# Products of the modulation weights and sums of the head norms in other places, and all low halves of the weights on VectorE for the middle of a hybrid attention block

## The chip, the cores and the metric

The kernel runs on one core of a Trainium2 chip. TensorE does the matmuls (PE in the profile, PEld its weight loads), VectorE (DVE), ScalarE (ACT) and GpSimd (POOL) work on tiles, and SyncE (SP) issues nearly all transfers. The metric is device time in microseconds, the median of several runs. The profile is that of one further execution.

## The reference

One layer of a diffusion backbone over 256 latent tokens and 256 context tokens, width 2048, all in float32:

```python
sh1, sc1, g1, sh2, sc2, g2 = split(silu(c) @ w_ada + b_ada, 6)        # and the same of c_ctx
h_l = modulate(rms_norm(x, norm1_w), sh1, sc1)                        # h_c from ctx
gq, gk, gv, gr, gaf, gab, dq, dk, dv = split(h @ w_in)                # for both token sets
ya = rms_norm(gla_scan(...)) * silu(gr)                               # gated linear attention, both directions
yb = rms_norm(diff_softmax(rope(rms_norm(dq)), [rms_norm(dk_c), rope(rms_norm(dk_l))], dv))
g_a, g_b = split(sigmoid(h_l @ w_gate + b_gate))
x = x + g1 * ((g_a * (ya @ w_proj_gla) + g_b * (yb @ w_proj_diff)) @ w_out)
h2 = modulate(rms_norm(x, norm2_w), sh2, sc2)
x = x + g2 * ((silu(gate) * val) @ w_down)       # gate, val = split(depthwise_conv3(h2 @ w_up))
```

`w_ada` is 2048 x 12288. Its first third (`sh1`, `sc1`) is needed at the start, `g1` at the output projection, `sh2` and `sc2` behind it, `g2` at the very end.

## The kernel before, in words

Activations lie transposed, channels on the 128 partitions. To keep float32 precision on TensorE every operand is written as a high half (the value rounded to the matmul's format) and a low half (the value less the high half), and three products are added: high x high, high x low and low x high.

**Weights.** `fetch` (line 224) loads 1024 columns of 128 rows, 512 KB, into one of four `wraw` buffers through SP. `split` (line 197) makes the halves of 512 of these columns: ScalarE copies the high half into `whi` (line 206), then the low half `wlo` is a subtraction (line 213) on VectorE, or on GpSimd for every `splits[1]`-th split. Each kind of half has four buffers. `splits[1]` is 0 in the first sweep, then 4 (`PSH` and `PSH2`, lines 39 and 40) for all the rest.

**Tiles.** `col_tile` (line 238) makes one 128-column tile of a weight times the 256 latent tokens: two fetches, four splits, and for each split a quad of four wide matmuls (`h0` to `h3`, 512 columns, high and low halves of the activations side by side, line 262) and four narrow ones with the low half of the weight (`l0` to `l3`, 256 columns, line 264). `col_tile2` does the same for both token sets with six matmuls per 128 rows, and `row_tile` (lines 275 to 277) puts the tokens on the partitions for the values.

**Modulation products.** The last two thirds of `w_ada` are not multiplied on TensorE. `ada_load` (line 326) brings 128 pieces of 128 x 1024 through SP, in program order, into two `araw` buffers, and `ada_dot` (line 334) multiplies one by the condition row and adds it up on VectorE (line 336). `ada_next(n)` (line 650) adds n to what is due and, for each whole piece due, does the oldest product when both buffers are taken, then loads the next. `ada_dot` is ordered behind VectorE's last low half, and VectorE works in order: a product whose weights have not landed holds up what stands behind it. `ada_done(j0)` (line 663) sees to it that the sixteen columns from j0 are finished.

**Norms of heads.** `heads_norm` (line 597) squares a finished query or key tile and appends the rest of its work to `later`; `flush` runs it when the next tile is at its second fetch. This rest splits the squares with `split`, adds them up over a head with two matmuls (`sums`, lines 594 and 595, tile `hss`) and normalizes.

**Stages**, with times of the profile: the first sweep (to 142 us); gated linear attention with its queries, keys and values and the other branch's keys (to 419); the value chunk 0 (`dv_chunk`, sixteen row splits with twelve matmuls each, tile `dvb`), four query tiles (`dq_tile`), the value chunk 1 (to 553); eight heads of differential attention, with three gate tiles behind each and the other four query tiles between, then eight gate tiles more (`gate_tile`, to 797); sixteen pairs of projection tiles (`pga`, `pgb`, to 886); sixteen output tiles (`mix`, to 978), behind whose half the second modulation begins; the first six up strips (`up`, to 1013), the others (`upg`, `upv`, to 1471), and the down tiles.

The order of the instructions on each engine is not the program's: a planner lays them out by simulated durations, `tc.high_priority` moves attention ahead, and only `tc.keep_in_program_order` and `after` bind.

Of the kernel before, what the change touches and what calls it, by code (L numbers as in the profile page):

```python
# [23 lines left out]
DK = 64  # L24
# [14 lines left out]
PSH2 = 4  # L39
# [1 line left out]
UPS = 6  # L41
SLOTS = 12
EARLY_ADA = 4, 14
GATE_ADA = [0.25] * 24 + [2] * 8
NRM = [(0, 0)] * 2 + [(j, j + 1) for j in range(12)] + [(12, 14), (14, 16)]

_VEC = {}
# [99 lines left out]
def layer_kernel(tc, I, out):  # L147
# [3 lines left out]
    with es:  # L151
# [5 lines left out]
        def acc_bank(name):  # L157
            return ps.tile([P, 512], F32, tag="acc", bufs=4, name=name)
# [33 lines left out]
        copied = [None, None]  # L192
        chain = []
        pin = [False]
        later = []

        def flush():
            while later:
                later.pop(0)()

        def split(raw, n, lows=None):

# [35 lines left out]
        def col_tile(src, acts, b, orders=None):  # L238

            nk = src.shape[1]
            nq = nk // 4
            tied = orders is not None
            orders = orders or [TURN] * (nq - 1) + [ENDED]
            for k0 in range(0, nk, 8):
                kn = min(8, nk - k0)
                if k0:  # L250
                    flush()
                raw = fetch(src[:, k0:k0 + kn, :].rearrange("p a b -> p (a b)"), kn * P)
                for kk in range(0, kn, 4):
                    whi, wlo = split(raw[:, kk * P:(kk + 4) * P], 4 * P)
                    order = orders[(k0 + kk) // 4]
                    for which in order:
                        j = int(which[1])
                        k = k0 + kk + j
                        sl = slice(j * P, (j + 1) * P)
                        first, last = k == 0 and which == "h0", k >= nk - 4 and which == order[-1]  # L260
                        if which[0] == "h":
                            i = PE.matmul(b.rearrange("p (a b) -> p a b", a=2), whi[:, sl], acts[k], start=first, stop=last)  # L262
                        else:
                            i = PE.matmul(b[:, T:], wlo[:, sl], acts[k][:, 1, :], start=False, stop=last)  # L264
                        if tied:
                            if chain:
                                after(i, chain[0])
                            chain[:] = [i]

        def added(dst, b):  # L270
            S.copy(dst, b[:, :T])
# [7 lines left out]
        def rsqrt_parts(y, t, ss, n, table=None):  # L279

            i = S.activation(y, ss, AF.Ln, scale=1.0 / n, bias=epsb)
            if table is not None:
                after(i, table)
            exps.append(S.activation(y, y, AF.Exp, scale=-0.5))
            S.activation(t, y, AF.Square)
            V.scalar_tensor_tensor(t, ss, n * EPS, t, op0=ALU.add, op1=ALU.mult)
# [6 lines left out]
        def normed_by(dst, src, w, y, t, n):  # L293
            V.scalar_tensor_tensor(dst, src, w, y, op0=ALU.mult, op1=ALU.mult)
            V.scalar_tensor_tensor(dst, t, -3.0 * n, dst, op0=ALU.add, op1=ALU.mult)
# [291 lines left out]
        def norm_tiles():  # L587
            return [tp.tile([P, 512], F32, tag=t, name=t) for t in ("nraw", "nsq", "hny")]

        def sums(o, m, sq, halves=None):  # L590

            n = sq.shape[1]
            hi, lo = halves or split(sq, n)
            i = PE.matmul(o, m, lo[:, :n], start=True, stop=False)
            after(PE.matmul(o, m, hi[:, :n], start=False, stop=True), i)

        def heads_norm(b, wname, done, o, sq, y):


            n = o.shape[1]  # L600
            if n == T:
                added(o, b)
                S.activation(sq, o, AF.Square)
            else:
                S.activation(sq, b, AF.Square)
                S.copy(o, b)

            def rest():
                s = acc_bank("hss")
                sums(s[:, :n], bones, sq)  # L610
                rsqrt_parts(y, sq, s[:, :n], DK)
                normed_by(o, o, wname, y, sq, DK)
                done(o)

            later.append(rest)

        def onormed(pool, dst, ob, w, halves=None, copy=V.tensor_copy):

# [54 lines left out]
        with tc.tile_pool(name="gla", bufs=1) as pg:  # L673
# [36 lines left out]
            def col_tile2(src, b):  # L710

                for k0 in range(0, KT, 8):
                    if k0:
                        flush()
                    raw = fetch(src[:, k0:k0 + 8, :].rearrange("p a b -> p (a b)"), 1024)
                    for kk in range(8):
                        if kk % 4 == 0:
                            whi, wlo = split(raw[:, kk * P:(kk + 4) * P], 512)
                        k = k0 + kk
                        both_tile(b, k, whi, wlo, slice(kk % 4 * P, (kk % 4 + 1) * P), k == 0, k == KT - 1)  # L720

            def dk_tile(h):
                ada_next(0.5)
# [167 lines left out]

            dk_done(0, sweep[6])
            flush()
            S.copy(gaT, gb[:96, :])
            V.tensor_tensor(gaT[32:64], gb[32:64, :], gaT[32:64].bitcast(F32), op=ALU.subtract)

# [26 lines left out]
        with tc.tile_pool(name="diff", bufs=1) as pd:  # L923
# [11 lines left out]
            def dv_chunk(j):  # L935
                banks = [acc_bank("dvb") for _ in range(4)]

                turn = [6, 7, 0, 1, 2, 3, 4, 5] if j else list(range(8))
                for q in turn:
                    if q == turn[1]:  # L940
                        flush()
                    raw = fetch(I["w_dv"][j, q].rearrange("p a b -> p (a b)"), 1024)
                    ada_next(2)
                    for a in range(2):
                        whi, wlo = split(raw[:, a * 512:(a + 1) * 512], 512)
                        k = 2 * q + a
                        for t in range(4):
                            hi, lo = H[t // 2]
                            row_tile(banks[t], k, whi, wlo, slice(0, 512), hi, lo, slice((t % 2) * P, (t % 2 + 1) * P),
                                     k == 2 * turn[0], k == 2 * turn[-1] + 1)  # L950
                for t in range(4):
                    S.copy(dv[:, t, 512 * j:512 * (j + 1)], banks[t])
# [76 lines left out]
                V.tensor_tensor(gates[j], b[:, T:], gates[j], op=ALU.add)  # L1029

            nts = norm_tiles()
            dv_chunk(0)
            for h in range(4):
                dq_tile(h)
# [43 lines left out]
        for c in range(KT):  # L1078
            ba, bb = acc_bank("pga"), acc_bank("pgb")
            col_tile(I["w_proj"][c, :, 0:8, :], yap, ba)  # L1080
            col_tile(I["w_proj"][c, :, 8:16, :], ybp, bb)
            for j in (c, 16 + c):
                sigs.append(S.activation(gates[j], gates[j], AF.Sigmoid))
                after(sigs[-1], sigm)
                after(sigs[-1], copied[0])
            for b, j in ((ba, c), (bb, 16 + c)):
                t = p3.tile([P, T], F32, tag="pt", bufs=2, name="pt")
                i = added(t, b)
                (G if j > c else V).tensor_tensor(gates[j], t, gates[j], op=ALU.mult)
                if j == c and c:  # L1090
                    merged(c - 1, i)
            ada_next(11 / 16)
        merged(KT - 1, i)
        splits[1] = PSH2
        ada_done(0)


# [19 lines left out]
        half = KT // 2  # L1117
        for c in range(KT):
            b = acc_bank("mix")
            col_tile(I["w_out"][c], A, b)  # L1120
            if c == half:
                ada_done(16)
                ada_done(32)
                V.tensor_scalar(a2, adav[:, 32:48], 1.0, None, op0=ALU.add)
                V.tensor_tensor(a2, a2, vcol("norm2", 0, 16), op=ALU.mult)
                V.tensor_scalar(a2, a2, -0.5 / D, None, op0=ALU.mult)
            xr = p3.tile([P, T], F32, tag="xr", bufs=2, name="xr")
            nc.scalar.dma_start(xr, I["xl"][:, c, :])
            x1.append(C[c][:, 0, :])
            V.scalar_tensor_tensor(xr, b[:, :T], adav[:, c:c + 1], xr, op0=ALU.mult, op1=ALU.add)  # L1130
            i = V.scalar_tensor_tensor(x1[c], b[:, T:], adav[:, c:c + 1], xr, op0=ALU.mult, op1=ALU.add)
            if c >= half:
                for k in range(2 * (c - half), 2 * (c - half) + 2):
                    unnormed(k, i, summed)
            sq = p3.tile([P, T], F32, tag="sq2" if c else "sq_sum", bufs=2 if c else 1, name="sq2")
            S.activation(sq, x1[c], AF.Square)
            if c == 0:
                sq_sum = sq
            elif c < KT - 1:
                summed = G.tensor_tensor(sq_sum, sq_sum, sq, op=ALU.add)  # L1140
# [42 lines left out]

        with tc.tile_pool(name="ffn", bufs=1) as pf:
            gs = []
            ada_buffers(st, 2)
            temps = [0]

# [66 lines left out]
```

## Time and profile before

| What | us |
|---|---|
| median of three runs (1722.74 to 1723.88) | 1723.04 |
| the profiled execution | 1721.52 |
| its span, first to last instruction | 1719.7 |
| TensorE busy | 1687.4 |
| VectorE busy | 1231.6 |
| ScalarE busy | 981.2 |
| GpSimd busy | 487.8 |

The page's lines give busy time, share of the span and the number of instructions. A matmul's end is modelled, so TensorE's 98% says that it seldom stops, not that it runs at its peak. In the groups a line reads: line, engine, operation, out<-in, count, then busy time and mean of one, then the engine's idle time before them and what ended it. In a timeline each row has its start, its length and, in brackets, the idle time ahead of it and who ended that. A row with the engine name SPq is a transfer being issued.

### The profile page before, as it was taken

Reading aid. Unit: us, or ns where it says so; the run is one execution under the profiler, and the core shown is the slowest. Engines: PE = TensorE matmul, PEld = TensorE weight load, DVE = VectorE, ACT = ScalarE, POOL = GpSimd, SP = SyncE. Lnnn points to the kernel's source line nnn. Section 1 sums busy time; section 2 is a strip of 40 time slices with the busy share of each in tenths; the row PEclk is TensorE's granted clock in tenths of the full one; section 3 lists DMA queues with packets and bytes.
Section 4 is the critical chain, followed back from the end, with each engine's and each line's share of the span. In section 5 each row is a group of like instructions: output and inputs, shape, how many; then the busy total and the mean of one; then the engine's idle time right before and its main releaser. Section 6 shows DMA issues by size and latency. Waiting matters only on the chain. (4 is left out here: it accounts for less than half of the span.)

```text
span 1719.7 us, 29261 instructions
## 1 busy us (share of the span) xinstructions
PE 1687.4 (98%) x10460; PEld 1462.9 (85%) x10460; DVE 1231.6 (72%) x2224; ACT 981.2 (57%) x1992; POOL 487.8 (28%) x474
## 2 busy tenths in 40 slices
PE   7999999999999999999999999999999999999999
PEld 5779999897777888878888998888888888888887
DVE  4556655868677888678987898788887777644443
ACT  5335555665355777656665576666666666444443
POOL 0002534645121222223443522222222222222222
PEclk9999999999999999999999999999999999999999
DMA  9995532435766555588776666666766666666664
GB/s 384 408 408 180 173 119 77 136 111 174 242 205 212 172 163 171 171 289 304 246 247 197 187 210 221 226 224 222 232 232 226 225 225 223 207 199 195 196 202 137
DMA packets 108451, 368.75 MB, mean 214 GB/s; under 512 B 12176, under 2 KB 17040, under 8 KB 108304
## 3 DMA queue, kind: packets, MB, share of 16 engines
q1 hardware_dynamic: 103264, 362.51, 63.7%
q10 hardware_dynamic: 5040, 4.37, 0.8%
q8 instruction: 82, 1.34, 0.3%
q14 instruction: 65, 0.53, 0.1%
HBM read 364.73 MB, written 2.10 MB: 213 GB/s over the span
## 5 line engine op out<-in xcount | busy, mean ns | idle before, releaser
L206 ACT CAST whi<-wraw 128x512 fp32r<-128x512 f32 (+2 forms) x1004 | 604.4, 608 | 384.7 <-PE down L262 111.3
L213 DVE TENSOR_TENSOR wlo<-wraw,whi 128x512 fp32r<-128x512 f32 (+2 forms) x761 | 527.9, 703 | 245.0 <-ACT whi L206 239.6
L213 POOL TENSOR_TENSOR wlo<-wraw,whi 128x512 fp32r<-128x512 f32 (+2 forms) x243 | 335.0, 1379 | 932.5 <-ACT whi L206 828.9
L262 PE MATMUL down<-g,whi 128*128 128x512 f32 x704 | 243.6, 392 | 0.0
L262 PE MATMUL upv<-a,whi 128*128 128x512 f32 x656 | 229.2, 392 | 0.0
L262 PE MATMUL upg<-a,whi 128*128 128x512 f32 x656 | 229.2, 392 | 0.0
L336 DVE CUSTOM_DVE_ANT_0 araw<-araw,cb 128x1024 f32<-128x1024 f32 x128 | 178.8, 1400 | 34.7 <-DMA araw<-in_w_ada 34.5
L264 PE MATMUL down<-g,wlo 128*128 128x256 f32 x704 | 195.4, 280 | 0.7 <-DVE wlo L213 0.7
L264 PE MATMUL upv<-a,wlo 128*128 128x256 f32 x656 | 183.1, 280 | 0.6 <-POOL wlo L213 0.3
L264 PE MATMUL upg<-a,wlo 128*128 128x256 f32 x656 | 182.8, 280 | 0.0
L262 PE MATMUL gate<-a,whi 128*128 128x512 f32 x512 | 181.3, 399 | 0.0
L262 PEld LDWEIGHTS down<-g,whi 128*128 128x128 f32 x704 | 131.0, 187 | 28.3
L262 PEld LDWEIGHTS upv<-a,whi 128*128 128x128 f32 x656 | 122.4, 187 | 26.6 <-ACT whi L206 0.2
L262 PEld LDWEIGHTS upg<-a,whi 128*128 128x128 f32 x656 | 122.4, 187 | 26.6
L264 PE MATMUL gate<-a,wlo 128*128 128x256 f32 x512 | 141.3, 286 | 3.1 <-DVE wlo L213 3.1
L264 PEld LDWEIGHTS down<-g,wlo 128*128 128x128 f32 x704 | 132.9, 189 | 1.9 <-DVE wlo L213 1.0
L264 PEld LDWEIGHTS upv<-a,wlo 128*128 128x128 f32 x656 | 123.9, 189 | 2.0 <-DVE wlo L213 0.9
L264 PEld LDWEIGHTS upg<-a,wlo 128*128 128x128 f32 x656 | 123.9, 189 | 1.1 <-DVE wlo L213 0.6
L262 PEld LDWEIGHTS gate<-a,whi 128*128 128x128 f32 x512 | 95.1, 189 | 20.2 <-ACT whi L206 0.8
L264 PEld LDWEIGHTS gate<-a,wlo 128*128 128x128 f32 x512 | 97.1, 190 | 10.1 <-DVE wlo L213 4.5
L262 PE MATMUL mix<-a,whi 128*128 128x512 f32 x256 | 89.0, 397 | 0.7 <-ACT whi L206 0.7
L1197 ACT ACTIVATE C<-C,vec 128x256 f32<-128x256 f32 x88 | 52.6, 598 | 29.1 <-DVE C L272 29.1
(332 smaller groups left out, 3394.2 us busy)
## 6 DMA issues: line engine op xcount, KB each, us to landing
wraw<-in_w_up SPq DMA_DIRECT2D x164, 512.0 KB, 4.4
araw<-in_w_ada SPq DMA_DIRECT2D x128, 512.0 KB, 4.9
wraw<-in_w_down SPq DMA_DIRECT2D x80, 512.0 KB, 3.9
ada<-in_w_ad SPq DMA_DIRECT2D x64, 512.0 KB, 9.9
wraw<-in_w_gate SPq DMA_DIRECT2D x64, 512.0 KB, 4.1
wraw<-in_w_in SPq DMA_DIRECT2D x58, 512.0 KB, 3.9
wraw<-in_w_proj SPq DMA_DIRECT2D x32, 512.0 KB, 4.9
wraw<-in_w_out SPq DMA_DIRECT2D x32, 512.0 KB, 4.2
```

The costliest lines, as they stand in the source:

```text
L206: copied[0] = S.copy(hi[:, :n], raw)
L213: i = e.tensor_tensor(lo[:, :n], raw, hi[:, :n].bitcast(F32), op=ALU.subtract)
L262: i = PE.matmul(b.rearrange("p (a b) -> p a b", a=2), whi[:, sl], acts[k], start=first, stop=last)
L264: i = PE.matmul(b[:, T:], wlo[:, sl], acts[k][:, 1, :], start=False, stop=last)
L336: i = V.tensor_tensor_reduce(raw, raw, cb[:, q * 1024:(q + 1) * 1024], 1.0, 0.0, op0=ALU.mult, op1=ALU.add, accum_out=ada2[:, j, q:q + 1])
L1197: S.activation(u, b, AF.Identity, bias=vcol("conv_b", ct), scale=vcol("conv_w", 2 * FT + ct))
```

## The change

Four edits:

- **Products later.** In the value chunks `ada_next` is now called once per split with 1, not once per fetch with 2, and in chunk 0 only from the fifth fetch on: 24 products in place of 32. The gates have 0.25 for nineteen tiles and 1.25 for thirteen, in place of 0.25 for 24 and 2 for eight: 21 in place of 22. The projections have 12 in place of 11. The first eight output tiles have one each, where there were none: 8.
- **Norms' sums later.** What `heads_norm` leaves over is cut in two. The split of the squares runs where all of it ran before; the two matmuls and the normalizing go to a second list, `latest`, which is run behind the first quad of the next tile's second fetch (in the value chunk, at the fetch after).
- **Low halves.** `splits[1]` becomes 0 ahead of value chunk 0 and 4 again ahead of the remaining up strips, so that from the value chunks to the first six up strips every low half is VectorE's.
- `sums` no longer splits by itself.

```diff
-GATE_ADA = [0.25] * 24 + [2] * 8
+GATE_ADA = [0.25] * 19 + [1.25] * 13
...
-        later = []
-
-        def flush():
-            while later:
-                later.pop(0)()
+        later, latest = [], []
+
+        def flush(work=later):
+            for step in [work.pop(0) for _ in range(len(work))]:
+                step()
...
                             if chain:
                                 after(i, chain[0])
                             chain[:] = [i]
+                    if k0 and not kk:
+                        flush(latest)
...
-        def sums(o, m, sq, halves=None):
+        def sums(o, m, sq, halves):
 
             n = sq.shape[1]
-            hi, lo = halves or split(sq, n)
+            hi, lo = halves
...
-            def rest():
-                s = acc_bank("hss")
-                sums(s[:, :n], bones, sq)
-                rsqrt_parts(y, sq, s[:, :n], DK)
-                normed_by(o, o, wname, y, sq, DK)
-                done(o)
-
-            later.append(rest)
+            def parts():
+                halves = split(sq, n)
+
+                def rest():
+                    s = acc_bank("hss")
+                    sums(s[:, :n], bones, sq, halves)
+                    rsqrt_parts(y, sq, s[:, :n], DK)
+                    normed_by(o, o, wname, y, sq, DK)
+                    done(o)
+
+                latest.append(rest)
+
+            later.append(parts)
...
                         both_tile(b, k, whi, wlo, slice(kk % 4 * P, (kk % 4 + 1) * P), k == 0, k == KT - 1)
+                        if k0 and kk == 3:
+                            flush(latest)
...
             dk_done(0, sweep[6])
             flush()
+            flush(latest)
...
                 for q in turn:
-                    if q == turn[1]:
-                        flush()
+                    if q in turn[1:3]:
+                        flush((later, latest)[turn.index(q) - 1])
                     raw = fetch(I["w_dv"][j, q].rearrange("p a b -> p (a b)"), 1024)
-                    ada_next(2)
                     for a in range(2):
+                        if j or q > 3:
+                            ada_next(1)
...
             nts = norm_tiles()
+            splits[1] = 0
             dv_chunk(0)
...
-            ada_next(11 / 16)
+            ada_next(12 / 16)
         merged(KT - 1, i)
-        splits[1] = PSH2
         ada_done(0)
...
             b = acc_bank("mix")
+            if c < half:
+                ada_next(1)
             col_tile(I["w_out"][c], A, b)
...
             gs = []
+            splits[1] = PSH2
             ada_buffers(st, 2)
```

## The prediction

> **What bounds the kernel now.** I read the page first, then the waits of TensorE alone, then the busy time by stage, then VectorE's timeline around the longest waits.
>
> ```profile
> span 1719.7 us, 29261 instructions
> ...
> PE 1687.4 (98%) x10460; PEld 1462.9 (85%) x10460; DVE 1231.6 (72%) x2224; ACT 981.2 (57%) x1992; POOL 487.8 (28%) x474
> ...
> L213 POOL TENSOR_TENSOR wlo<-wraw,whi 128x512 fp32r<-128x512 f32 (+2 forms) x243 | 335.0, 1379 | 932.5 <-ACT whi L206 828.9
> ```
>
> TensorE is busy nearly all the time, so no rearrangement gains more than its idle time and the time in which it ran slowly. Its own waits say who ends them:
>
> ```profile
> PE dvb L277 <- DVE wlo L213: 3.1, 2, 1.7
> PE gate L264 <- DVE wlo L213: 3.1, 2, 2.5
> PE o L863 <- DVE at L854: 2.5, 1, 2.5
> PE hss L594 <- DVE wlo L213: 1.3, 1, 1.3
> PE hss L594 <- DVE rc L756: 1.3, 1, 1.3
> ...
> PE gr L264 <- DVE wlo L213: 1.1, 2, 0.9
> PE dq L262 <- ACT whi L206: 0.9, 2, 0.5
> PE pT L1006 <- DVE ont L286: 0.9, 1, 0.9
> ...
> PE mix L262 <- ACT whi L206: 0.7, 1, 0.7
> ```
>
> Nearly all name VectorE, and 14.9 us stand here. Now the stages (columns: length, busy us and count of PE, PEld, DVE, ACT, POOL, then the granted clock and the DMA share and rate):
>
> ```profile
> 391.60:395.00 3.40, 3.24 (x10) 2.76 (x11) 3.32 (x7) 1.36 (x3) 0.00 (x0) 0.50 0.34 75
> 767.10:770.40 3.30, 3.30 (x12) 2.82 (x11) 1.86 (x4) 0.69 (x2) 1.41 (x1) 0.50 0.91 340
> 500.00:553.00 53.00, 49.85 (x230) 38.91 (x228) 44.40 (x86) 23.18 (x48) 8.47 (x6) 1.00 0.76 245
> 553.00:720.00 167.00, 166.08 (x956) 139.44 (x954) 133.65 (x276) 122.27 (x270) 41.80 (x35) 1.00 0.51 168
> 797.00:886.50 89.50, 89.33 (x507) 77.00 (x506) 83.59 (x143) 62.00 (x142) 41.24 (x31) 1.00 0.74 253
> 886.50:932.00 45.50, 45.50 (x260) 39.53 (x259) 30.40 (x47) 23.50 (x43) 15.85 (x16) 1.00 0.71 230
> 1013.00:1470.60 457.60, 457.03 (x2630) 401.23 (x2629) 372.82 (x657) 298.72 (x596) 116.49 (x82) 1.00 0.70 226
> ```
>
> The last row, the up strips, has no slack: its 2630 matmuls are 82 column tiles of 32, so a tile takes 457.6 / 82 = 5.58 us: sixteen matmuls 512 wide at 0.23 us and sixteen half as wide. The first two show something the list of waits hides: twice a pause was followed by some 3.3 us at clock 0.50, in which half the work was done, about 1.7 us lost each time. The projections (797 to 886.5) are where VectorE is nearest its limit, 83.59 of 89.5, and TensorE still hardly waits there: 93% busy is borne.
>
> **The change, part by part.** *(a) The first value chunk* loses its products before q = 4. There the pair's last mask copies stood behind products that waited for their weights:
>
> ```profile
> 439.25 1.23 DVE L336 CUSTOM_DVE_ANT_0 araw<-araw,cb 128x1024 f32<-128x1024 f32 x1 [1.89 <-DMA araw<-in_w_ada]
> ...
> 441.67 1.23 DVE L336 CUSTOM_DVE_ANT_0 araw<-araw,cb 128x1024 f32<-128x1024 f32 x1 [1.19 <-DMA araw<-in_w_ada]
> ...
> 443.91 0.48 PE L863 MATMUL o<-at,gv 128*128 128x256 f32 x1 [2.48 <-DVE at L854]
> ```
>
> The two waits and two products are 1.89 + 1.23 + 1.19 + 1.23 = 5.5 us of VectorE ahead of L854; without them the 2.5 us pause goes. Next late would be the factors from ScalarE, which the copies need too. SP's loads that go with these products go later as well, so w_dv fetches no longer queue behind loads that wait for a product. I take -2.5, bounds 0 and -2.5.
>
> *(b) The second value chunk* keeps 16 products, but one per split (one in 2.76 us of matmuls, twelve of 0.23) instead of two per fetch. With two buffers a load still has only two splits, 5.5 us, until its product. The two pauses (3.1 us) each stood behind a pair of products; single ones hold up a low half by half as much. I take -1.5, bounds 0 and -3.1.
>
> *(c) The gates.* Eight tiles with two products each become thirteen with 1.25. First the loads' row of the DMA view from 746 to 797 us (its last number: from issue to landing), then VectorE's timeline there:
>
> ```profile
> araw<-in_w_ada SPq DMA_DIRECT2D x15, 512.0 KB, 5.9
> ```
>
> ```profile
> 761.42 1.23 DVE L336 CUSTOM_DVE_ANT_0 araw<-araw,cb 128x1024 f32<-128x1024 f32 x1 [1.90 <-DMA araw<-in_w_ada]
> 762.57 0.42 DVE L1029 TENSOR_TENSOR C<-gate,C 128x256 f32<-128x256 f32 x1
> 764.49 1.23 DVE L336 CUSTOM_DVE_ANT_0 araw<-araw,cb 128x1024 f32<-128x1024 f32 x1 [1.50 <-DMA araw<-in_w_ada]
> 765.64 0.08 DVE L336 DVE_READ_ACCUMULATOR2_ANT ada<- 128x1 f32 x1
> 765.64 1.89 DVE L213 TENSOR_TENSOR wlo<-wraw,whi 128x512 fp32r<-128x512 f32 x3
> ```
>
> Here a load lands after 5.9 us, while two buffers at two products a tile give it one tile, 5.58: every product waits, and the low halves (0.63 each) queue behind. At 1.25 a tile it has 8.9 us. VectorE then needs 4 x 0.63 + 0.42 + 1.25 x 1.31 = 4.6 of 5.58 us a tile. Of 3.1 us idle and 1.7 us of half clock I take -4.5, bounds 0 and -4.8. The Trainium skill (TensorE: Matmul & The Clock Gate, "Why this matters for your kernels") puts the danger at idle gaps over about 3 us; by it only the 3.1 would be had here. The trace disagrees: the pause was 2.5 us by the waits, and the clock row shows 0.50 behind it.
>
> *(d) The norms' sums* go behind one more quad of matmuls, while their split stays in its place. At stake are both hss waits (2.6), the gr wait behind one (0.9) and the half clock at 391.6 (1.7): 5.2 us. But the split still stands ahead of the next quad's low half on VectorE, and if the planner keeps that order TensorE waits for that low half instead:
>
> ```profile
> 388.26 1.76 DVE L213 TENSOR_TENSOR wlo<-nsq,whi 128x512 fp32r<-128x512 f32 x1
> ...
> 389.44 1.72 POOL L213 TENSOR_TENSOR wlo<-wraw,whi 128x512 fp32r<-128x512 f32 x1
> ...
> 389.95 1.76 DVE L213 TENSOR_TENSOR wlo<-wraw,whi 128x512 fp32r<-128x512 f32 x1
> ```
>
> The low half ends at 391.7 either way; and the norm's halves hold one of four high and one of four low buffers for a quad more. I take -1.5, bounds +1 (the quad now waits through both) and -5.2.
>
> *(e) Low halves by VectorE alone.* From the value chunks to the first strips there are 360 splits (32 value, 32 + 8 query, 128 gate, 64 + 64, 32); every fourth, 90, leaves GpSimd. Each adds 0.63 us to VectorE. What it takes away is seen here, where a subtraction that lasts 0.68 alone stood beside a GpSimd one:
>
> ```profile
> 507.43 0.68 DVE L232 TENSOR_TENSOR ks<-dk,ks 128x512 fp32r<-128x512 f32 x1
> ...
> 602.62 1.48 POOL L213 TENSOR_TENSOR wlo<-wraw,whi 128x512 fp32r<-128x512 f32 x1
> 602.86 1.77 DVE L232 TENSOR_TENSOR ks<-dk,ks 128x512 fp32r<-128x512 f32 x1
> ...
> 605.03 0.66 PE L1006 MATMUL pT<-ident,pe 128*128 128x128 f32 x4 [0.90 <-DVE ont L286]
> ```
>
> The 1.1 us of stretch there became the pT pause. In the projections, VectorE's costliest groups (after the bar: busy us, mean ns), an A subtraction that stood alone, and the busy time of L213 alone on VectorE and GpSimd:
>
> ```profile
> L336 DVE CUSTOM_DVE_ANT_0 araw<-araw,cb 128x1024 f32<-128x1024 f32 x11 | 21.1, 1920 | 2.1 <-DMA araw<-in_w_ada 2.1
> L213 DVE TENSOR_TENSOR wlo<-wraw,whi 128x512 fp32r<-128x512 f32 x46 | 32.2, 725 | 0.8 <-ACT whi L206 0.8
> L232 DVE TENSOR_TENSOR a<-C,a 128x256 fp32r<-128x256 f32 x14 | 10.2, 730 | 0.0
> ```
>
> ```profile
> 884.73 0.42 DVE L232 TENSOR_TENSOR a<-C,a 128x256 fp32r<-128x256 f32 x1
> ```
>
> ```profile
> 797.00:886.50 89.50, 32.21 (x46) 26.30 (x16) 1.00 0.74 253
> ```
>
> Stretch: 11 x (1.92 - 1.23) + 14 x (0.73 - 0.42) + 46 x (0.725 - 0.68) = 7.6 + 4.3 + 2.1 = 14.0 us. Splits are 26.30 of GpSimd's 41.24 us, so 8.9 us go with them, 0.56 a split. VectorE: 83.59 + 16 x 0.63 + 1.3 (one product more) - 8.9 = 86.1 of 89.5: covered, if closely. Attention (some 24 gate and 4 query tiles, so a quarter of 116 splits): 133.65 + 29 x (0.63 - 0.56) = 135.7 of 167. In the shorter waits of the query, pT and mix rows (2.5) I take -1.0, bounds 0 and -2.5. The Trainium skill (SBUF — State Buffer, "Who interferes with whom") says that a VectorE instruction with two SBUF inputs and a GpSimd one that reads SBUF lock each other out for a whole instruction; the rows above agree, and by the rule at its fullest 16 x 1.64 = 26 us would be freed.
>
> *(f) The output tiles* get eight products, one a tile, and SP one load each ahead of a w_out fetch. First half: 30.40 + 8 x 0.63 + 8 x 1.31 = 45.9 of 45.5 us, less 8 x 0.56 = 4.5: 41.4, or 91%. A load has two tiles, 11.2 us, to land, so the product itself should not wait; if it does, low halves queue behind it, TensorE runs on what lies in four buffers (four quads, 5.58 us), and SP holds the next w_out fetch behind the load that needs the product's buffer. With the closeness in (e): +1.5, bounds 0 and +6 (below nothing not: work is added).
>
> Sum: -2.5 - 1.5 - 4.5 - 1.5 - 1.0 + 1.5 = -9.5 us. The profiled execution took 1721.52 (its span and 1.8 us around it), so 1712.0; the median of the runs, 1723.04, lies 1.5 higher, so 1713.5.
>
> **Rivals.** *Slower: VectorE overflows in the projections.* If taking the splits off GpSimd frees nothing there, VectorE needs 83.59 + 10.1 + 1.3 = 95.0 of 89.5 us: 5.5 us come to TensorE, and 0.4 in (f). Pauses of about 2 us were enough for a half clock twice; three such add 5.1. Against 11.0 stand (a) and (c), 7.0, the parts that need no relief: +4.0, 1727. It decides at a relief under 5.5 / 16 = 0.34 us a split, against my 0.56. For it: VectorE is the nearest to full there. Against: 1.92 for a product that takes 1.23 elsewhere. The Trainium skill (Perfetto Trace Analysis, "Optimizing Scalar/DVE Operations") speaks for this rival: it would give work of a saturated VectorE to another engine, even GpSimd; it adds that the shared read port may undo that, and the trace bears out the addition.
>
> *No change: the pauses come back elsewhere.* All orders are the planner's, which prices instructions by itself and lays out every stage anew. If in (a) and (b) the low halves are still late behind products that wait for weights, (d) gives nothing and (f) costs 3, there is left -4.5 - 1.0 + 3 = -2.5: 1720.5. For it: (b) leaves a load 5.5 us.
>
> *The sums are not really later.* The planner may put them, or the next quad's wait, where they were: (d) is 0, 1715.
>
> **How the numbers follow.** Two runs' difference can be told from none at about 0.2%, 3.4 us. My forecast, 1713.5, own range 1708 to 1718: 0.50. Sums unmoved, 1715: 0.12. No change, 1720.5: 0.22. Overflow, 1727: 0.16. So faster 0.62, within 0.2% 0.22, slower 0.16. The range goes from 1708.0, with (b), (c) and (d) at their full bounds (15.1 us gained), to 1726.5, just short of the overflow.
>
> **What would show it.** Right: no pause at the o matmuls before the middle of the first value chunk; no half clock near the last gates; VectorE's product near 1.3 us in the projections and VectorE at 84 to 88 us there; GpSimd's L213 count down by 90 to 153. Wrong: new TensorE waits on wlo in the projections or output tiles, products waiting for weights in the first eight output tiles, or the value chunks as long as now (500 to 553).

## The result and the profile after

The changed kernel takes 1706.16 us (median, 1705.33 to 1706.62) against 1722.89 for the kernel before: 0.9899 of its time, 95% interval 0.9885 to 0.9914, so 17 us less where 9.5 were forecast. It lies 1.8 us below the range's lower end. The profiled execution took 1705.99 us, 15.5 less than that of before. Its page begins:

```profile
span 1704.2 us, 29160 instructions
...
PE 1680.4 (99%) x10460; PEld 1461.5 (86%) x10460; DVE 1236.4 (73%) x2314; ACT 983.8 (58%) x1992; POOL 373.4 (22%) x384
...
L213 POOL TENSOR_TENSOR wlo<-wraw,whi 128x512 fp32r<-128x512 f32 (+1 forms) x155 | 208.2, 1343 | 644.9 <-ACT whi L206 572.2
```

GpSimd has 90 instructions fewer and VectorE 90 more (two of them were norms' low halves, so the weights' group falls by 88). VectorE took on 90 subtractions, and its busy time rose by 4.8 us only. TensorE's idle time (span less busy) fell from 32.3 to 23.8 us and its busy time by 7.0; the two half clocks of before are some 3.4 of the 7.0, and where the rest lay was not traced. TensorE's own waits, in the same view as before:

```profile
PE gr L264 <- DVE wlo L213: 2.7, 4, 1.6
PE hss L596 <- DVE wlo L213: 1.2, 1, 1.2
PE gr L264 <- POOL wlo L213: 1.1, 1, 1.1
PE mix L264 <- DVE wlo L213: 1.0, 1, 1.0
...
PE dq L264 <- DVE wlo L213: 0.6, 2, 0.4
...
PE dvb L277 <- ACT whi L206: 0.6, 1, 0.6
...
PE gate L264 <- DVE wlo L213: 0.5, 1, 0.5
...
PE dvb L279 <- DVE wlo L213: 0.2, 1, 0.2
```

The waits of the value chunks, the gates, the o and the pT matmuls are gone or small; what is left stands mostly in the attention part ahead of them (gr, hss). The stages, with the columns as before:

```profile
417.30:467.90 50.60, 50.60 (x253) 41.29 (x252) 33.29 (x65) 17.96 (x35) 9.31 (x15) 1.00 0.54 177
496.00:549.90 53.90, 53.14 (x253) 42.01 (x252) 44.23 (x91) 27.53 (x59) 1.47 (x2) 1.00 0.73 246
549.90:714.00 164.10, 164.10 (x949) 139.03 (x948) 136.63 (x300) 120.31 (x262) 9.90 (x10) 1.00 0.54 177
767.00:771.00 4.00, 4.00 (x25) 3.50 (x24) 3.04 (x5) 1.50 (x3) 0.00 (x0) 1.00 0.91 323
780.30:871.00 90.70, 90.70 (x521) 79.29 (x520) 86.95 (x164) 63.60 (x144) 19.52 (x15) 1.00 0.76 250
871.00:917.00 46.00, 44.98 (x256) 38.89 (x255) 40.21 (x69) 23.50 (x42) 9.59 (x7) 1.00 0.89 305
```

The granted clock is 1.00 near the last gates (767 to 771) and everywhere else up to the end. The row from 496.00 to 549.90 runs to the first gate, behind the second value chunk's end; from the first start of that chunk's matmuls to the last it was 55.6 us before and is 53.0 now. Where the time went is read from the first start of each stage's matmuls (the tile view: shortest, median and longest in ns, then first and last start). Before:

```profile
L275 PE MATMUL dvb<-whi,a x64: 387/389/500, 419.1 to 550.6; 128*128 128x512 f32 x64
...
L262 PE MATMUL dq<-a,whi x128: 387/395/505, 471.8 to 647.3; 128*128 128x512 f32 x128
...
L262 PE MATMUL gate<-a,whi x512: 387/395/628, 559.5 to 795.7; 128*128 128x512 f32 x171
...
L262 PE MATMUL pga<-ya,whi x128: 387/395/400, 794.5 to 883.7; 128*128 128x512 f32 x128
...
L262 PE MATMUL mix<-a,whi x256: 389/395/495, 886.5 to 978.2; 128*128 128x512 f32 x128
```

After:

```profile
L277 PE MATMUL dvb<-whi,a x64: 387/389/580, 417.3 to 541.2; 128*128 128x512 f32 x64
...
L262 PE MATMUL dq<-a,whi x128: 387/395/497, 467.9 to 635.5; 128*128 128x512 f32 x128
...
L262 PE MATMUL gate<-a,whi x512: 387/395/500, 549.9 to 781.5; 128*128 128x512 f32 x171
...
L262 PE MATMUL pga<-ya,whi x128: 392/394/398, 780.3 to 868.2; 128*128 128x512 f32 x128
...
L262 PE MATMUL mix<-a,whi x256: 387/395/403, 871.0 to 962.8; 128*128 128x512 f32 x128
```

By differences: up to the value chunks 1.8 us gained, the first chunk 2.1, the queries and the second chunk 5.7, heads and gates 4.6, projections 1.3, and from the output tiles to the end nothing (both take 833.2 us from the first mix matmul to the last instruction: 1719.7 - 886.5 and 1704.2 - 871.0). But the planner also moved work over these borders: sixteen sc matmuls of linear attention went into the first chunk (24 with 1.88 us there before, 40 with 3.04 after), and six s matmuls (1.0 us) behind the first gate. For the same work the gains are some 0.6, 3.3, 4.7, 5.6 and 1.3 us.

### The profile page after: what moved, and what is told of

Same layout as the page of the kernel before. It is cut to its first block, busy times and chain, and to the rows that moved or that the text cites. A ratio compares the mean times of both kernels' runs of the same rounds, so it can differ in the third digit from the quotient of the medians.

```text
span 1704.2 us, 29160 instructions
## 1 busy us (share of the span) xinstructions
PE 1680.4 (99%) x10460; PEld 1461.5 (86%) x10460; DVE 1236.4 (73%) x2314; ACT 983.8 (58%) x1992; POOL 373.4 (22%) x384
## 3 DMA queue, kind: packets, MB, share of 16 engines
q8 instruction: 82, 1.34, 0.3%
## 4 chain that ended last, share of the span: by engine, by line
PE 90%; DVE 5%; DMA 3%; ACT 1%; issue 1%; POOL 0%; DVEq 0%; ACTq 0%
PE down L262 9%; PE upg L262 8%; PE upv L262 8%; PE gate L262 7%; PE sweep L350 5%; PE down L264 5%; PE upg L264 4%; PE upv L264 4%; PE gate L264 4%; PE mix L262 3%; PE ab L350 2%; DMA araw<-in_w_ada 2%; PE mix L264 2%; PE pga L262 2%; PE pgb L262 2%; PE dk L313 1%
## 5 line engine op out<-in xcount | busy, mean ns | idle before, releaser
L213 DVE TENSOR_TENSOR wlo<-wraw,whi 128x512 fp32r<-128x512 f32 (+2 forms) x849 | 588.7, 703 | 236.8 <-ACT whi L206 228.7
L213 POOL TENSOR_TENSOR wlo<-wraw,whi 128x512 fp32r<-128x512 f32 (+1 forms) x155 | 208.2, 1343 | 644.9 <-ACT whi L206 572.2
L338 DVE CUSTOM_DVE_ANT_0 araw<-araw,cb 128x1024 f32<-128x1024 f32 x128 | 163.7, 1282 | 15.2 <-DMA araw<-in_w_ada 15.2
L264 PE MATMUL mix<-a,wlo 128*128 128x256 f32 x256 | 69.3, 281 | 1.0 <-DVE wlo L213 1.0
```

The lines of the kernel that those rows point to most:

```text
L213: i = e.tensor_tensor(lo[:, :n], raw, hi[:, :n].bitcast(F32), op=ALU.subtract)
L338: i = V.tensor_tensor_reduce(raw, raw, cb[:, q * 1024:(q + 1) * 1024], 1.0, 0.0, op0=ALU.mult, op1=ALU.add, accum_out=ada2[:, j, q:q + 1])
```

## The experiments

Each ran five rounds against the kernel before; a ratio's interval is 95%. Microseconds behind a ratio are its distance from 1 times 1724.

**Runs 1 to 4: the parts alone.** Three parts are switched one by one: the products' places, the norms' sums, the low halves. Each kernel has the lines of the change's diff that belong to its parts and is otherwise the kernel before.

Run 1, products only. 

> Only the places of the products are changed; sums and low halves stay as before. Theory 1 (the gain comes from products that no longer stand ahead of low halves with their weights still on the way; GpSimd's splits cost little): 7 to 11 us under the kernel before, with the pauses at the o matmuls, in the second value chunk and in the last gates gone. Theory 2 (half of the gain or more comes from VectorE no longer being held up beside GpSimd): at most 6 us, with pauses left in the second value chunk and new ones in the first eight output tiles.

Measured: 0.9961 (0.9949 to 0.9973), 6.7 us less. That is just short of theory 1 and just over theory 2's bound, and decides nothing. Among TensorE's waits of this run a pause is left in the second value chunk (pT), and the output tiles wait a little longer for low halves than the 0.2 us of before:

```profile
PE pT L1007 <- DVE pe L1004: 1.3, 1, 1.3
...
PE mix L264 <- DVE wlo L213: 0.7, 2, 0.4
```

From their first to their last start the output tiles' matmuls take 93.3 us here and 92.9 in run 11, against 91.7 before:

```profile
L262 PE MATMUL mix<-a,whi x256: 387/395/501, 879.5 to 972.8; 128*128 128x512 f32 x128
```

Run 2, sums only. 

> Only the sums of the head norms go behind one more quad. Theory 1: 1 to 2.5 us under the kernel before, all of it ahead of the first value chunk (hss waits and the half clock there). Theory 2: the planner's order moves the wait to the next low half: within 1 us of the kernel before.

Measured: 0.9986 (0.9978 to 0.9995), 2.4 us less: theory 1's size. The half clock ahead of the value chunks is gone from its profile, but not all of the gain stays: in the first value chunk an sc matmul waits 2.6 us, and behind it the granted clock averages 0.68 from 440 to 444 us.

Run 3, low halves only:

```diff
             nts = norm_tiles()
+            splits[1] = 0
             dv_chunk(0)
...
-        splits[1] = PSH2
         ada_done(0)
...
             gs = []
+            splits[1] = PSH2
```

> Only the low halves go to VectorE from the value chunks to the first up strips; products and sums stay. Theory 1: 1 to 3 us under the kernel before, and VectorE's products in the projections near 1.3 us instead of 1.9. Theory 2: 5 us or more under it, the pauses of the second value chunk gone though the products still come in pairs.

Measured: 0.994 (0.9926 to 0.9954), 10.3 us less (7.9 to 12.8). Theory 1, the prediction's, falls here: it gave the low halves 1 to 3 us, and they alone do at least as much as the products. The trace shows how, at one place where VectorE has the same instructions in the same order up to the low half that TensorE waits for. Before, VectorE and GpSimd at the start of the second value chunk, then TensorE's wait:

```profile
502.57 1.75 DVE L336 CUSTOM_DVE_ANT_0 araw<-araw,cb 128x1024 f32<-128x1024 f32 x1
503.84 1.64 POOL L213 TENSOR_TENSOR wlo<-wraw,whi 128x512 fp32r<-128x512 f32 x1 [0.59 <-ACT whi L206]
...
504.40 2.16 DVE L336 CUSTOM_DVE_ANT_0 araw<-araw,cb 128x1024 f32<-128x1024 f32 x1
...
507.23 0.73 PE L277 MATMUL dvb<-wlo,a 128*128 128x512 f32 x2 [1.46 <-DVE wlo L213]
```

And in run 3:

```profile
501.47 1.76 DVE L336 CUSTOM_DVE_ANT_0 araw<-araw,cb 128x1024 f32<-128x1024 f32 x1
...
503.21 1.23 DVE L336 CUSTOM_DVE_ANT_0 araw<-araw,cb 128x1024 f32<-128x1024 f32 x1
...
505.10 0.73 PE L277 MATMUL dvb<-wlo,a 128*128 128x512 f32 x2 [0.26 <-DVE wlo L213]
```

The pair of products still stands ahead of the low half. But the second one takes 1.23 us, not 2.16, now that no GpSimd subtraction runs beside it, and the pause shrinks from 1.46 to 0.26. The prediction had put this pause down to the pair, and that was not wrong either: in run 1 one product stands there, the GpSimd subtraction is still beside it and even lengthens the low half (1.77 us for 0.68), and the pause is as small:

```profile
499.74 1.75 DVE L336 CUSTOM_DVE_ANT_0 araw<-araw,cb 128x1024 f32<-128x1024 f32 x1
501.01 1.63 POOL L213 TENSOR_TENSOR wlo<-wraw,whi 128x512 fp32r<-128x512 f32 x1 [0.60 <-ACT whi L206]
...
501.42 1.77 DVE L213 TENSOR_TENSOR wlo<-wraw,whi 128x512 fp32r<-128x512 f32 x1
...
503.25 0.74 PE L277 MATMUL dvb<-wlo,a 128*128 128x512 f32 x2 [0.31 <-DVE wlo L213]
```

The pause needed both causes. Theory 2's sign, no pause in the second value chunk, did not come true: a product that waited for its weights held up a softmax step there, TensorE paused for longer than at any place of that chunk before, and behind it the granted clock averaged 0.60 from 533.4 to 537.7 us:

```profile
531.40 1.23 DVE L336 CUSTOM_DVE_ANT_0 araw<-araw,cb 128x1024 f32<-128x1024 f32 x1 [2.51 <-DMA araw<-in_w_ada]
...
533.36 0.66 PE L1006 MATMUL pT<-ident,pe 128*128 128x128 f32 x4 [2.85 <-DVE pe L1003]
```

By first starts this run's profile gains nothing in the queries and the second chunk (87.9 us against 87.7), but about 5 in heads and gates, 1.2 in the projections and 1.9 behind them.

Run 4, products and low halves. 

> Products and low halves as in the changed kernel, sums as before. Theory 1: the two gains add, and 1 to 2.5 us are missing to the changed kernel. If the sums need both (or do nothing), it equals the changed kernel within 1 us.

Measured: 0.9908 (0.9894 to 0.9923), 15.9 us less (13.3 to 18.3). The two alone make 17.0: a sum, as far as the noise lets one see.

**Runs 5 to 7 and 9: what the low halves are worth, and by which way.** Run 5 is the changed kernel with the three `splits[1]` lines as before. 

> All of the change except the low halves: every fourth one stays on GpSimd. The theory left after the first four runs is that the low halves are the largest part, some 9 us whatever else is changed: 7 to 9 us under the kernel before. Rival: products and low halves remove the same pauses, so that either of them does most of it: 12 us or more under it.

Measured: 0.9947 (0.9934 to 0.996), 9.1 us less. The whole change makes 17.4, so the low halves are worth some 8 us on top of all the rest: the theory's size, and the rival falls.

Run 6 has run 3's low halves, and run 7 the changed kernel's, with this besides, between the same two places:

```diff
             else:
                 lows.append(low)
+            if idle[0] and splits[0] % PSH == 0:
+                G.tensor_tensor(raw, raw, hi[:, :n].bitcast(F32), op=ALU.subtract)
             return hi, lo
```

> Low halves on VectorE as in the third run, but GpSimd still does its quarter of the subtractions for nothing: after VectorE's low half it subtracts the high half once more from the raw weight in place, and nobody uses the result. If VectorE's slowness beside GpSimd is what cost the time, most of the 10 us is lost again: at most 4 us under the kernel before, VectorE's products in the projections again at 1.7 us or more. If it was the lateness of the low halves that GpSimd made, 7 us or more remain.

> The changed kernel with the same idle subtractions on GpSimd. By slowness beside GpSimd: 6 us or more above the changed kernel, with the output tiles' first half over its time (46 us of VectorE in 45.5). By lateness of the low halves: within 3 us of the changed kernel.

Measured: run 6 1.0134 (1.0118 to 1.0151) and run 7 1.0096 (1.008 to 1.0111): 23 and 17 us slower than the kernel before, 33 and 34 us slower than the same kernels without the idle work. Nobody waits for its result, yet 90 such instructions cost about 0.37 us each. That is not what GpSimd's quarter cost in the kernel before: there VectorE had 90 subtractions less to do beside it.

Run 9 tells whether it is the reading or the buffer that the instruction keeps from being refilled. It is run 7 with `for _ in range(3): G.memset(raw, 0.0)` in place of the subtraction. 

> The changed kernel, and GpSimd behind every fourth low half writes zeros three times over the used-up raw weight (three writes to come near the length of one subtraction): the same hold on the raw buffer as in the seventh run, but nothing is read by GpSimd. If VectorE's slowness beside a reading GpSimd was the 33 us of the seventh run, nearly all of it goes: within 6 us of the changed kernel and VectorE's products again near 1.25 us. If the held raw buffers (later fetches) were it: 20 us or more above.

Measured: 0.992 (0.9907 to 0.9933), 3.6 us above the changed kernel, not 34. GpSimd was nearly as long at it and kept the weights nearly as long (SP waited 135.9 us for it before refilling them, 177.2 in run 7). GpSimd's costliest group between the value chunks and the up strips, run 7:

```profile
L225 POOL TENSOR_TENSOR wraw<-wraw,whi 128x512 f32<-128x512 f32 (+1 forms) x88 | 155.2, 1763 | 268.5 <-DVE wlo L214 245.5 <-DVE sm L1008 12.9 <-issue 7.5
```

Run 9:

```profile
L226 POOL MEMSET wraw<- 128x512 f32 (+1 forms) x264 | 136.4, 517 | 268.3 <-DVE wlo L214 258.8
```

VectorE's products in the same stretch (count, busy us, mean ns): the kernel before, run 1, run 3, run 7 and run 9.

```profile
L336 DVE CUSTOM_DVE_ANT_0 araw<-araw,cb 128x1024 f32<-128x1024 f32 x69 | 100.3, 1459 | 34.0 <-DMA araw<-in_w_ada 33.9
```

```profile
L336 DVE CUSTOM_DVE_ANT_0 araw<-araw,cb 128x1024 f32<-128x1024 f32 x71 | 101.2, 1430 | 12.8 <-DMA araw<-in_w_ada 12.4
```

```profile
L336 DVE CUSTOM_DVE_ANT_0 araw<-araw,cb 128x1024 f32<-128x1024 f32 x69 | 85.7, 1246 | 31.9 <-DMA araw<-in_w_ada 31.6
```

```profile
L341 DVE CUSTOM_DVE_ANT_0 araw<-araw,cb 128x1024 f32<-128x1024 f32 x71 | 99.9, 1415 | 9.2 <-DMA araw<-in_w_ada 9.2
```

```profile
L342 DVE CUSTOM_DVE_ANT_0 araw<-araw,cb 128x1024 f32<-128x1024 f32 x71 | 89.6, 1268 | 11.8 <-DMA araw<-in_w_ada 11.6
```

The two edits separate here. Moving the products (run 1) takes away their waits for weights, 33.9 to 12.4 us, and leaves them long. Moving the low halves (run 3) leaves the waits and makes them short. GpSimd subtractions (run 7) make them long again, GpSimd writes (run 9) don't: 1.27 us. Run 9 differs from run 7 in one thing more: its memsets do not hold the high half's buffer. In run 7 ScalarE waited 9.4 us for that; but VectorE waited no longer for high halves ahead of its low halves than in the changed kernel (20.2 us against 26.3, from the value chunks to the up strips), while the low halves themselves rose from 0.71 to 0.82 us each, so this explains little of the 34.

A memset reads nothing from SBUF, which is the exception that the Trainium skill (SBUF — State Buffer, "Who interferes with whom") names for a VectorE instruction with two inputs there; these two runs agree with it.

**Runs 10 to 13: where in the kernel.** Run 10 has of the products only `GATE_ADA` and the projections' 12; run 11 only the value chunks' places and the output tiles' eight. 

> Of the products only the gates' 1.25 in thirteen tiles (and 12 in place of 11 in the projections); value chunks and output tiles as before, sums and low halves as before. Step (c) of the prediction: 3 to 5 us under the kernel before, with no half clock near the last gates.

> Of the products only the value chunks' (one per split, none before the fifth fetch of chunk 0) and, to make up for it, one in each of the first eight output tiles. Steps (a), (b) and (f): -2.5 - 1.5 + 1.5, so 2 to 4 us under the kernel before; the first half of the output tiles 1 to 2 us longer than before.

Measured: run 10 0.998 (0.997 to 0.9989), 3.4 us; run 11 0.997 (0.9957 to 0.9983), 5.2 us. The second is more than the prediction's three terms, although the output tiles took the 1.2 us more that (f) had expected.

Run 12 sets `splits[1]` back to `PSH` ahead of the projections; run 13 sets it to 0 only there. 

> Low halves on VectorE from the value chunks to the last gates; from the projections on every fourth on GpSimd again; products and sums as before. 60 of the 90 splits with the softmax work beside: if the gain goes with the pauses that stood in this part, 7 to 8 of the 10 us. If it goes with the fullness of VectorE (the projections), 3 us or less.

> The counterpart of the twelfth run: low halves on VectorE only from the projections to the first up strips, 30 of the 90; products and sums as before. If the parts add, 10 less 6.4: about 4 us under the kernel before. If they overlap, 1 us or less.

Measured: run 12 0.9963 (0.9951 to 0.9975), 6.4 us; run 13 0.9984 (0.9974 to 0.9995), 2.8 us. They add up to 9.2 of the 10.3. The numbers of splits in both expectations were miscounted: it is 50 (32 + 40 + 128 splits, a quarter) up to the gates and 40 behind. A split is worth 0.13 us (0.09 to 0.17) where softmax and norms run beside it and 0.07 (0.02 to 0.11) in the projections and output tiles. The two are not clearly apart, but nothing shows a larger gain in the projections, where VectorE is fullest.

**Runs 8 and 14: a better version.** Run 8 is the changed kernel with `splits[1] = 0` already where it was set to `PSH` at the start of the attention part; run 14 also leaves it 0 for the up and down tiles. 

> The changed kernel with VectorE making the low halves in the stage of gated linear attention too (142 to 417 us), where GpSimd has 30 of them and other work beside. If a GpSimd split costs more than the 0.63 us that VectorE needs for it, there too: 1 to 4 us under the changed kernel. If GpSimd's other work there keeps the port busy anyway: within 1 us of it.

> The changed kernel with every low half of the whole kernel on VectorE, the up and down tiles' 126 too. There TensorE has no pauses but some 1 us at the first up strips: within 2 us of the eighth run (0.987 of the kernel before), the best version so far or its equal. If VectorE (371 us busy of 457 in the up tiles, 82 x 0.63 more) comes to its limit: slower than the eighth run by over 2 us.

Measured: run 8 0.9872 (0.9857 to 0.9888), 1701.23 us; run 14 0.9855 (0.9843 to 0.9868), 1698.7 us, the fastest of all. Run 8 is 4.9 us under the changed kernel, a little more than the 1 to 4 expected, and run 14 is 2.5 us under run 8, where 2 was the most expected; the intervals of these two overlap. With no split on GpSimd at all, the kernel takes 25 us less than the one before.

## Why the prediction was too small

It forecast faster, and it is faster; the size was off by 8 us, and the term that was mis-sized is (e), the low halves.

- *(a), (b), (f), products of the chunks and output tiles:* -2.5 - 1.5 + 1.5 = -2.5 forecast, -5.2 alone (run 11). The pause at the o matmuls went as described; the first chunk is some 3.3 us shorter for the same work. The cost of (f) came where GpSimd still splits, 1.6 us in run 1 and 1.2 in run 11 by the output tiles' first and last starts. In the changed kernel it did not: they take 91.8 us for 91.7, with one new wait of 1.0 us for a low half; VectorE had 40.21 of 46.0 us in their first half, 41.4 of 45.5 forecast.
- *(c), gates:* -4.5 forecast, -3.4 alone (run 10), and some 5.6 us of heads and gates in the changed kernel, the half clock included. But the same pause all but went in run 3 too, where two products a tile stayed: there the gates wait 0.4 and 1.0 us, not 0.6 and 2.5:

```profile
PE gate L264 <- DVE wlo L213: 1.5, 2, 1.0
```

  So here too either edit alone was enough. The two products ahead of the pause before (761.42 and 764.49) were not lengthened, 1.23 us each. Whether in run 3 it was the missing subtractions or the planner's other order of VectorE there (a low half between the two products) was not taken apart.
- *(d), sums:* -1.5 forecast, -2.4 alone (0.9 to 3.8), some 0.6 in the changed kernel up to the value chunks for the same work. The half clock at 391.6 is gone, while the waits moved to the gr tile's low halves (2.7 + 1.1 us), as feared.
- *(e), low halves:* -1.0 forecast, 0 to -2.5 as bounds; -10.3 alone, -8 on top of the rest. The step that failed is: "VectorE: 83.59 + 16 x 0.63 + 1.3 (one product more) - 8.9 = 86.1 of 89.5: covered, if closely". The sum in it was good, 86.95 measured, as was the attention's 135.7 (136.63), and VectorE's relief is 83.59 + 10.1 + 1.3 - 86.95 = 8.0 us, 0.50 a split, against 0.56 taken and 0.34 at which the overflow would have begun. (The window after holds 64 low halves, that of before 62, so the relief is rather larger.) In the projections, after the change:

```profile
L338 DVE CUSTOM_DVE_ANT_0 araw<-araw,cb 128x1024 f32<-128x1024 f32 x12 | 15.6, 1303 | 0.9 <-DMA araw<-in_w_ada 0.9
...
L232 DVE TENSOR_TENSOR a<-C,a 128x256 fp32r<-128x256 f32 x14 | 5.8, 413 | 0.0
```

What was wrong is the inference from it: as much work added as taken away, so nothing gained but three short waits. What stops TensorE is not the sum of VectorE's busy time but what stands ahead of one low half at the moment when it is wanted. The 0.63 us that came fall due where the low half is wanted; the 0.5 us that went stood as stretches of up to 1.1 us in front of other low halves and softmax steps, and both pauses of (b) were in part theirs: 0.93 of the 1.46 us is the second product's, and ahead of the other pause, 1.69 us at 546.08, a softmax step that takes 0.75 alone took 1.77 beside a GpSimd subtraction. For (c) that isn't shown. The row that showed it was quoted, the ks subtraction of 1.77 us ahead of the pT pause, and priced for that one wait. The upper bound, 2.5, counted only waits that no other part had claimed; but pauses with two causes went with either edit, and of run 3's gain 3.1 us came from the projections on, where the rows of waits before show only 0.9 that went (mix). Where the rest of the 3.1 us stood is open.

Whether the gains overlap is not shown: run 1's and run 3's make 17.0 where run 4 has 15.9, and the low halves make 10.3 alone and 8 on top of the rest, both within the noise. The overflow rival had its premise refuted (0.50 a split against 0.34), as had the one of pauses coming back: of the 14.9 us in the rows of TensorE's waits shown for before, the rows shown for after have 7.9, and 5.0 of these (gr and hss) stand ahead of the value chunks.

## What to carry to other kernels

Price a helper engine not by what it takes off the busy one but by how long each of the busy one's instructions becomes beside it, and look for the stretched ones just ahead of the waits of the engine that sets the time. Equal sums of busy time can hide that. When two causes stand ahead of one pause, undo each alone before giving the pause to either.

## What the runs showed of the hardware

A VectorE instruction with two SBUF operands beside a GpSimd one that reads SBUF was lengthened by up to 1.1 us (0.68 to 1.77), and idle GpSimd subtractions cost the changed kernel 34 us where idle GpSimd writes of nearly the same length (136.4 against 155.2 us busy) cost 3.6. The half clock of TensorE came, in the kernel before, behind a pause of 2.51 us and behind two of 1.34 and 0.95 close together, but not behind the one of 2.48 us at the o matmuls; in run 3 it came behind one of 2.85, too. None came in the changed kernel's profile from the first stage to the last, and its runs lie within 1.3 us of each other, where those of run 3, whose profile has a mean clock of 0.997, lie within 7.0. That these two go together is seen, not shown.
